# Decoder layer on one core: every engine keeps the source's order around the down projection, its weights are asked for two flushes ahead, and the next matrix's first four units go chunk by chunk

## The chip, the cores and the metric

One NeuronCore of a Trainium2 chip. The metric is the device time of one launch in microseconds (us); the kernel before was run three times, 2031.71, 2032.97 and 2035.16 us, median 2032.97.

## The reference: what is computed

One layer over 1056 tokens (a prompt of 1024 and 8 samples of 4), width 1024, in float32:

```
x = x + 1/2 * SwiGLU_1(RMSNorm(x))          # D_FF = 2816; gate, up, down
z = RMSNorm(x) @ w_in                       # q | k | v | gate B | gate C | h
x = x + concat([attention, short conv]) @ w_out
x = x + 1/2 * SwiGLU_2(RMSNorm(x))
x = x + sigmoid(RMSNorm(x) @ w_ple_gate) * (p @ w_ple_proj)
```

The parts around the change are the two down projections, and what follows each: `w_in` behind the first, `w_ple_gate` behind the second.

## The kernel before

**Numbers.** Each float32 operand is split into a high part (a cast on ACT) and a low part (a subtraction on DVE); a product is three matmuls, high x high, low x high, high x low. The gated matrices go through a scheme of seven products per 2x2 block of operands ("operations", in the order 1, 5, 2, 6, 7, 3, 4), so operands and results are also summed in blocks.

**Gate and up.** `gate_up` walks 22 column blocks j, each in two token halves c. A `segment` gives PE the seven products of a block (L446 to L448) and beside them drains the block before: casts, tanh (L578), products with the gate (L579, L600 to L605, on DVE, and L602 on POOL). The results' sums and splits (`hop_steps`, and `hop_last` for the last pair) go to a DRAM buffer `hop`.

**Down.** Two gate-up blocks make a pair, eleven in all; a pair comes back from `hop` as seven tiles of 528 KB (`load`, L875, by POOL's DMA queue) into four slots. FLUSH cuts the 44 products of a row block with a pair into 17 flushes of one to three pairs; each flush runs in two token halves (`DownQuad`, L828 to L830) and its results are added into X, on ACT the first time (L837), later on DVE (L839). A flush's weights (`DownWeights`) are four DMAs on SP's queue (L793), four sums on POOL (L797 to L800) and seven splits (ACT cast L364, DVE subtraction L365). They are asked for, summed and split in the second half of the flush ahead. In eight of the 17 flushes POOL also adds the residual into two rows of X (L882).

**Behind it.** The rows of X that are done are squared and summed, and their normalised splits are made (`prep`, L296 on ACT and L297 on DVE). The next matrix goes in units of 1024 columns: DMA to `wraw` (L172), cast (L182, ACT), subtraction (L183, DVE), then `proj` (L336 to L338) over three token chunks. `norm_r` sums the squares (L312 to L316), runs a chain of small DVE operations for the inverse root (L255 to L265), spreads it over the partitions with matmuls (L324) and hands it to k, v and q (L1092, L1132, L1157).

**The order.** All of it is written in Python in one order, but a scheduler inside the tile framework, with its own estimate of times, sets the order of the instructions of each engine. An engine works through its list in that order; a waiting instruction holds up all behind it.

Of the kernel before, what the change touches and what calls it, by code (L numbers as in the profile page):

```python
# [14 lines left out]
P = 128  # L15
# [6 lines left out]
FF = 22  # L22
# [48 lines left out]
DRAW = 42496  # L71

# [27 lines left out]
def tile_decoder_layer(  # L100
# [67 lines left out]
    def pump_dma():  # L168
        while st["dma"] < st["end"] and st["dma"] < st["split"] + RAW:
            i = st["dma"]  # L170
            t = at("wraw", (URAW2 if 2 <= i < 26 else URAW)[i % 2], 1024)
            nc.sync.dma_start(out=t, in_=units[i])  # L172
            raws[i] = t
            st["dma"] += 1
# [29 lines left out]
    def tick(split=True):  # L204
        now[0] += 1
        if split and can_split():
            split_one()
        while queue and min(queue)[0] <= now[0]:
            run_first()

# [324 lines left out]
    def hop_last(pr, c, src):  # L535
# [5 lines left out]
        def parts(u, n, hi, t, neg=False):  # L541
# [11 lines left out]
            lambda: parts(3, 2, new(), cell["a"]),  # L553
            lambda: parts(5, 2, new(), cell["b"], True),
# [54 lines left out]
    def lead_group(w, j, c, g):  # L609
# [20 lines left out]
        for h in range(2):  # L630
            ps = halfmm(1, h)
            nc.vector.tensor_tensor(out=g[:, h], in0=ps[:, :HH], in1=g[:, h], op=ALU.mult)
            if h:
                nc.sync.dma_start(out=hd[j, :, c * HC:(c + 1) * HC], in_=g.rearrange("p i t -> p (i t)"))
            yield

# [90 lines left out]
    def gate_up(gu, g, lw, steps, down):  # L727
# [36 lines left out]
        for j in range(LEAD, FF):  # L764
            for c in range(2):
                q = GateUp(w, j, c)
                if c:
                    q.follow = w = Weights(gu, j + 1) if j + 1 < FF else down.weights(0)
# [17 lines left out]
    class DownWeights(Weights):  # L786
        def __init__(self, dn, row, p0, p1):
            n = self.n = (p1 - p0) * P
            r = []
            for i in range(4):  # L790
                t = at("dr", DRAW + 384 * (dn_[0] % 6), 384)[:, :n]
                dn_[0] += 1
                nc.sync.dma_start(out=t, in_=dn[row, i, :, p0 * P:p1 * P])  # L793
                r.append(t)
# [71 lines left out]
    class Down:  # L866
# [3 lines left out]
        def weights(self, i):  # L870
            return DownWeights(self.dn, *FLUSH[i])
# [12 lines left out]
        def first(self, q):  # L884
# [7 lines left out]
            else:  # L892
                q.then = {
                    3: [lambda: ld(2, 1, 5, 2, 6)],
                    4: [lambda: ld(2, 7, 3, 4)],
                }

        def run(self, prev):
            w = prev.follow
# [36 lines left out]
            segment(None, prev)  # L936

# [93 lines left out]
    def norm_hook(g, xm):  # L1031

        def hook(r, ch):
            for m in (r, r + 4):
                for c in ((0,), (1, 2))[ch]:
                    square(c, m)
                if ch == 0:
                    prep(0, m, g)
                elif xm:
                    nc.sync.dma_start(out=xm_d[:, m], in_=X[m])  # L1040
            if r == 0 and ch == 1:
                for c in (1, 2):
                    for k in KORD:
                        prep(c, k, g)
        return hook

    dp = Down(w1d, xin, norm_hook(GM, True), 2)
    dp.run(gate_up(w1gu, G1, lw1, chunk1_steps(G1), dp))
    st["end"] = 26

# [100 lines left out]
    nc.gpsimd.memset(msq, 1.0)  # L1151
# [188 lines left out]
    nst = [norm_r(c, "nm", 9) for c in range(3)]  # L1340
    for c in range(3):
        ps = proj(U0, c)
        nst[c][0]()
        if c == 2:
            wdone(U0)
        ps1 = proj(U0 + 1, c)
        nst[c][1]()
        k_evac(c, ps)
        tick()
        v_evac(c, ps1)  # L1350
        tick()
    wdone(U0 + 1)
    for i in range(4):
# [4 lines left out]
        wdone(U0 + 2 + i)  # L1358

# [150 lines left out]
    dp = Down(w2d, xs_d, norm_hook(GP, False), 28)  # L1510
    dp.run(gate_up(w2gu, G2, lw2, chunk1_steps(G2), dp))
    st["end"] = 34
# [25 lines left out]
    for m in range(4):  # L1538
        ple_proj(m)
    nst = [norm_r(c, "np", 9) for c in range(3)]  # L1540
    for c in (0, 1):
        for m in (0, 1):
            ple_gate(m, c)
            nst[c][m]()
    ple_gate(0, 2)
    wdone(UG)
    nst[2][0]()
    for c in (0, 1):
        ple(0, c)
    ple_gate(1, 2)  # L1550
    wdone(UG + 1)
    nst[2][1]()
    ple(0, 2)
    for c in range(3):
        ple(1, c)
    for m in range(2, 8):
# [109 lines left out]
```

## Time and profile before

| | us |
|---|---|
| runs: lowest, median, highest | 2031.71, 2032.97, 2035.16 |
| the profiled execution's own time | 2034.04 |
| its span in the trace | 2032.3 |
| PE, DVE, ACT, POOL busy | 1955.5, 1375.5, 769.4, 912.6 |
| granted TensorE clock, mean | 0.978 |

The first down projection runs from 526 to 795 us, the second from 1683 to 1945. The span is what the trace covers; 1.7 us lie outside it. Busy shares are averages over stages with different limits, and what counts is which wait ends last in a stage.

### The profile page before, as it was taken

To read this page: it belongs to the slowest core of one execution; us is meant where nothing else is said; L and a number is where in the kernel's file an instruction comes from. 1 tells how busy PE (TensorE), PEld (TensorE's weight loads), DVE (VectorE), ACT (ScalarE), POOL (GpSimd) and SP (SyncE) were. 2 spreads that over 40 slices of the span, in tenths; PEclk is the share of its full clock that TensorE was granted. 3 is DMA by queue.
4 is the path that set the end of the run, shared out by engine and by line. 5 is a ranking of instruction groups with operands and counts; after the bars stand their busy time and mean duration, and the time that the engine had idled before them with its cause. 6 is when DMAs were issued, how large, how long until landed. Compare 5 with 4: busy or idle time off the path is not lost.

```text
span 2032.3 us, 38555 instructions
## 1 busy us (share of the span) xinstructions
PE 1955.5 (96%) x14639; PEld 1904.3 (94%) x14639; DVE 1375.5 (68%) x2571; ACT 769.4 (38%) x1654; POOL 912.6 (45%) x912
## 2 busy tenths in 40 slices
PE   7999999999899997999999799999999998999999
PEld 7999999999799997999887799999999997999998
DVE  6848877776467686456685357588777764777864
ACT  5324444444332233313344233344444434322521
POOL 2426665655456464002221125366565555565500
PEclk7999999999899998999999899999999999999999
DMA  6225754454988735101012331365445469986231
GB/s 240 85 67 189 244 168 143 136 165 132 365 293 265 242 117 173 35 22 33 31 32 86 106 105 48 113 214 183 138 152 163 127 222 317 295 295 194 93 128 50
DMA packets 189548, 315.46 MB, mean 155 GB/s; under 512 B 20801, under 2 KB 121545, under 8 KB 189236
## 3 DMA queue, kind: packets, MB, share of 16 engines
q1 hardware_dynamic: 164852, 224.55, 34.5%
q0 software_dynamic: 23648, 87.28, 12.6%
q8 instruction: 115, 1.88, 0.4%
q10 hardware_dynamic: 864, 1.18, 0.2%
q14 instruction: 69, 0.57, 0.1%
HBM read 204.66 MB, written 109.99 MB: 155 GB/s over the span
## 4 chain that ended last, share of the span: by engine, by line
PE 82%; DMA 6%; DVE 6%; issue 2%; POOL 2%; ACT 1%; SPq 0%; DVEq 0%; POOLq 0%; ACTq 0%
PE ps L446 11%; PE ps L447 11%; PE ps L448 11%; PE ps L828 7%; PE ps L830 7%; PE ps L829 7%; PE ps L336 4%; PE ps L338 4%; PE ps L337 4%; PE ps L1388 2%; PE ps L1389 2%; PE ps L1387 2%; PE ps L620 2%; PE ps L619 2%; PE ps L621 2%
## 5 line engine op out<-in xcount | busy, mean ns | idle before, releaser
L446 PE MATMUL ps<-bh_a,wh_a 128*128 128x264 f32 x2128 | 602.9, 285 | 4.7 <-DVE g_a L600 2.1
L447 PE MATMUL ps<-bh_a,wl_a 128*128 128x264 f32 x2128 | 604.3, 285 | 0.0
L448 PE MATMUL ps<-bl_a,wh_a 128*128 128x264 f32 x2128 | 599.6, 284 | 0.0
L446 PEld LDWEIGHTS ps<-bh_a,wh_a 128*128 128x128 f32 x2128 | 399.1, 188 | 7.4 <-DVE g_a L600 3.2
L447 PEld LDWEIGHTS ps<-bh_a,wl_a 128*128 128x128 f32 x2128 | 400.0, 188 | 0.0
L448 PEld LDWEIGHTS ps<-bl_a,wh_a 128*128 128x128 f32 x2128 | 399.9, 189 | 0.0
L828 PE MATMUL ps<-pair_a,vh_a 128*128 128x264 f32 x1232 | 355.9, 292 | 25.2 <-ACT x_a L837 8.8
L829 PE MATMUL ps<-pair_a,vl_a 128*128 128x264 f32 x1232 | 353.3, 288 | 0.0
L830 PE MATMUL ps<-pair_a,vh_a 128*128 128x264 f32 x1232 | 352.8, 288 | 0.0
L828 PEld LDWEIGHTS ps<-pair_a,vh_a 128*128 128x128 f32 x1232 | 234.6, 191 | 31.7 <-ACT x_a L837 10.3
L829 PEld LDWEIGHTS ps<-pair_a,vl_a 128*128 128x128 f32 x1232 | 236.4, 192 | 0.3 <-DVE vl_a L365 0.2
L830 PEld LDWEIGHTS ps<-pair_a,vh_a 128*128 128x128 f32 x1232 | 235.3, 191 | 0.0
L839 DVE SCALAR_TENSOR_TENSOR x_a<-ps,x_a 128x264 f32<-128x264 f32 x412 | 171.3, 425 | 90.4 <-PE ps L830 79.1
L336 PE MATMUL ps<-xnh_a,whi_a 128*128 128x384 f32 (+1 forms) x528 | 174.6, 331 | 12.9 <-DVE x_a L1479 7.0
L337 PE MATMUL ps<-xnh_a,wlo_a 128*128 128x384 f32 (+1 forms) x528 | 172.7, 328 | 0.0
L338 PE MATMUL ps<-xnl_a,whi_a 128*128 128x384 f32 (+1 forms) x528 | 172.7, 329 | 0.0
L365 DVE TENSOR_TENSOR wl_a<-ws_a,wh_a 128x512 fp32r<-128x512 f32 x152 | 131.8, 867 | 35.7 <-ACT wh_a L364 35.2
L389 POOL TENSOR_TENSOR ws_a<-wr_a,wr_a 128x512 f32<-128x512 f32 x38 | 50.8, 1336 | 213.0 <-DMA wr_a<-in_w2gu_dram 82.7
L364 ACT CAST wh_a<-ws_a 128x512 fp32r<-128x512 f32 x152 | 94.4, 621 | 99.9 <-PE ps L448 86.5
L364 ACT CAST vh_a<-dws_a 128x384 fp32r<-128x384 f32 (+2 forms) x136 | 63.1, 467 | 171.7 <-PE ps L830 139.2
L365 DVE TENSOR_TENSOR wl_a<-wr_a,wh_a 128x512 fp32r<-128x512 f32 x114 | 108.5, 954 | 12.8 <-ACT wh_a L364 11.6
L336 PEld LDWEIGHTS ps<-xnh_a,whi_a 128*128 128x128 f32 x528 | 102.0, 193 | 15.9 <-DVE x_a L1479 8.6
(268 smaller groups left out, 4166.8 us busy)
## 6 DMA issues: line engine op xcount, KB each, us to landing
pair_a<-hop POOLq DMA_DIRECT2D x154, 528.0 KB, 7.6
hop<-sg_a SPq DMA_DIRECT2D x240, 264.0 KB
wr_a<-in_w1gu_dram SPq DMA_DIRECT2D x88, 256.0 KB
wr_a<-in_w2gu_dram SPq DMA_DIRECT2D x88, 256.0 KB
hop<-sge_a SPq DMA_DIRECT2D x80, 132.0 KB
wraw_a<-in_win_dram SPq DMA_DIRECT2D x18, 512.0 KB
dr_a<-in_w1d_dram SPq DMA_DIRECT2D x44, 192.0 KB
dr_a<-in_w2d_dram SPq DMA_DIRECT2D x44, 192.0 KB
```

Source lines behind the costliest of these rows:

```text
L336: nc.tensor.matmul(ps[:, :W], lhsT=wh, rhs=xh, start=(k == 0), stop=False)
L337: nc.tensor.matmul(ps[:, :W], lhsT=wl, rhs=xh, start=False, stop=False)
L338: nc.tensor.matmul(ps[:, :W], lhsT=wh, rhs=xl, start=False, stop=(k == n - 1))
L364: nc.scalar.copy(out=hi, in_=src)
L365: nc.vector.tensor_tensor(out=lo, in0=src, in1=hi.bitcast(F32), op=ALU.subtract)
L446: nc.tensor.matmul(ps[:, :HH], lhsT=wh[:, ks], rhs=bh, start=(start and k == 0), stop=False, skip_group_check=True)
L447: nc.tensor.matmul(ps[:, :HH], lhsT=wl[:, ks], rhs=bh, start=False, stop=False, skip_group_check=True)
L448: nc.tensor.matmul(ps[:, :HH], lhsT=wh[:, ks], rhs=bl, start=False, stop=last, skip_group_check=True)
L828: nc.tensor.matmul(ps[:, :HH], lhsT=wh[:, ks], rhs=bh, start=(start and i == 0), stop=False, skip_group_check=True)
L829: nc.tensor.matmul(ps[:, :HH], lhsT=wl[:, ks], rhs=bh, start=False, stop=False, skip_group_check=True)
L830: nc.tensor.matmul(ps[:, :HH], lhsT=wh[:, ks], rhs=bl, start=False, stop=(i == n - 1), skip_group_check=True)
L839: nc.vector.scalar_tensor_tensor(out=x, in0=ps[:, :HH], scalar=f, in1=x, op0=ALU.mult, op1=ALU.add)
```

## The change

Between the first half of the last gate-up block and the end of the next matrix's first units, the scheduler is switched off: each engine gets its instructions as the Python code writes them (`in_order`). So that this order is usable, several things move in the code: a flush's weight DMAs go out two flushes ahead (flush 0 into four tiles of its own, `dr0`), apart from their sums; pairs 2 and 3 are loaded in the second halves of flushes 0 and 2 operation by operation, in place of the end of gate-up and of flush 0; the last pair's source is loaded a flush earlier and its last split delayed by five steps; the first unit of the next matrix is asked for after flush 15, and four units are in flight in place of two. The four first units are then worked as chunk 0 of all four, chunk 1, chunk 2 (`first_units`), in place of unit by unit; the splits of chunks 1 and 2 of X move from the end of the last flush into it. Line numbers shift by up to 72.

```diff
+            t = at("wraw", 30624 if i in (0, 26) else (URAW2 if 4 <= i < 26 else URAW)[i % 2], 1024)
...
             lambda: parts(3, 2, new(), cell["a"]),
+            *[lambda: None] * 5,
             lambda: parts(5, 2, new(), cell["b"], True),
...
+                if j == FF - 1 and c == 0:
+                    in_order(True)
                 if j == FF - 1:
                     down.first(q)
+                    if c:
+                        down.w[0].sums()
+                        down.w[1] = down.weights(1)
                 segment(q, prev)
                 prev = q
+                if j == FF - 2 and c:
+                    down.w = {0: down.weights(0)}
...
-            else:
-                q.then = {
-                    3: [lambda: ld(2, 1, 5, 2, 6)],
-                    4: [lambda: ld(2, 7, 3, 4)],
-                }
...
                     if c and i + 1 < len(FLUSH):
-                        nxt = self.weights(i + 1)
-                    done = (lambda r=f[0], c=c: self.hook(r, c)) if last_row[f[0]] == i else None
+                        nxt = self.w[i + 1]
+                        nxt.sums()
+                    done = (lambda r=f[0], c=c: self.hook(r, c)) if last_row[f[0]] == i and f[0] else None
                     q = DownQuad(w, c, f, done)
                     if c:
                         q.follow = nxt
+                        if i in (0, 2):
+                            for o in UNITS:
+                                q.then[o] = [lambda pr=2 + i // 2, o=o: self.load(pr, o)]
...
+                    if i in (4, 5) and c:
+                        src = from_hd(10, i - 4)
                     if i in (5, 6) and c == 0:
-                        hops.extend(hop_last(10, i - 5, from_hd(10, i - 5)))
+                        hops.extend(hop_last(10, i - 5, src))
+                    if i == len(FLUSH) - 1 and c:
+                        q.then[2] = [split_one]
...
-                    if i == 0 and c:
-                        self.load(3, 1, 5, 7, 2, 6, 3, 4)
-                    if i == len(FLUSH) - 1:
-                        if c == 0:
-                            st["end"] = self.end
-                            pump_dma()
-                        else:
-                            split_one()
+                    if c and i + 2 < len(FLUSH):
+                        self.w[i + 2] = self.weights(i + 2)
+                    if (i, c) in ((len(FLUSH) - 2, 1), (len(FLUSH) - 1, 0)):
+                        st["end"] = self.end - 3 * c
+                        pump_dma()
                 w = nxt
             segment(None, prev)
+            self.hook(0, 0)
+            split_one()
+            self.hook(0, 1)
...
+    def first_units(U, name, g, evac):
...
+        a = group(0, 0)
+        nst[0][0]()
+        split_next()
+        b = group(1, 0)
+        nst[0][1]()
+        preps(1, 0)
+        evac(0, 0, a)
+        evac(1, 0, b)
+        split_next()
+        a = group(2, 0)
+        preps(1, 1)
+        nst[1][0]()
+        evac(2, 0, a)
+        a = group(3, 0)
+        nst[1][1]()
+        evac(3, 0, a)
+        for u in range(4):
+            a = group(u, 1)
...
+    first_units(U0, "nm", GM, kvq_evac)
...
+    in_order(False)
```

Three places show the moved instructions; a row is line, operation, output and inputs (a name, its address, its number) and size.

First, ACT as the first down projection starts. Before: `sgl` is the cast of the last pair's source, which comes by DMA into `hd0`; `th` is the tanh of the last gate-up block; `x_a` is a down result; `vh` are weight splits.

```order
L364 CAST vh_a33728_6111<-dws_a41344_6017 128x128
L837 ACTIVATE x_a0_72<-ps_6153 128x264
L364 CAST vh_a34752_6177<-dws_a41728_6018 128x128
L364 CAST vh_a39424_6206<-dws_a42112_6019 128x128
L837 ACTIVATE x_a0_72<-ps_6153 128x264
L364 CAST sgl_a40192_6896<-hd0_6892 128x264
L578 ACTIVATE th_a48720_626<-g_a47664_1041 128x264
L364 CAST vh_a32704_6232<-dr_a43648_6014 128x128
```

The same place now:

```order
L370 CAST vh_a33728_6121<-dws_a41344_6019 128x128
L585 ACTIVATE th_a48720_626<-g_a47136_897 128x264
L869 ACTIVATE x_a0_72<-ps_6163 128x264
L370 CAST vh_a34752_6187<-dws_a41728_6020 128x128
L869 ACTIVATE x_a0_72<-ps_6163 128x264
L585 ACTIVATE th_a48720_626<-g_a47664_1041 128x264
L370 CAST vh_a39424_6216<-dws_a42112_6021 128x128
L370 CAST vh_a32704_6234<-dr0_a8304_5891 128x128
```

The cast `sgl` stood ahead of the last tanh; it now stands 67 rows behind it.

Second, POOL at the same place. Before: `pair_a` are the tiles of the pairs, their address telling pair and operation (23232 to 29568 and 44800, 45856 are pairs 2 and 3; 12672 and 13728 are operations 3 and 4 of pair 0); `dws` are the weight sums.

```order
L602 TENSOR_TENSOR g_a46608_779<-g_a46608_779,u_5932 128x264
L875 DMA pair_a23232_6210<-hop_76 128x1056
L875 DMA pair_a24288_6212<-hop_76 128x1056
L875 DMA pair_a44800_6297<-hop_76 128x1056
L875 DMA pair_a19008_6074<-hop_76 128x1056
L875 DMA pair_a20064_6076<-hop_76 128x1056
L875 DMA pair_a25344_6214<-hop_76 128x1056
L875 DMA pair_a26400_6216<-hop_76 128x1056
L798 TENSOR_TENSOR dws_a41344_6017<-dws_a40960_6016,dr_a42496_6008 128x128
L799 TENSOR_TENSOR dws_a41728_6018<-dr_a42496_6008,dr_a43264_6012 128x128
L875 DMA pair_a45856_6299<-hop_76 128x1056
L875 DMA pair_a12672_6131<-hop_76 128x1056
```

The same place now:

```order
L609 TENSOR_TENSOR g_a46608_779<-g_a46608_779,u_5942 128x264
L829 TENSOR_TENSOR dws_a40960_6018<-dr0_a8176_5889,dr0_a8304_5891 128x128
L830 TENSOR_TENSOR dws_a41344_6019<-dws_a40960_6018,dr0_a7920_5885 128x128
L831 TENSOR_TENSOR dws_a41728_6020<-dr0_a7920_5885,dr0_a8176_5889 128x128
L832 TENSOR_TENSOR dws_a42112_6021<-dws_a41344_6019,dr0_a8048_5887 128x128
L907 DMA pair_a19008_6084<-hop_76 128x1056
L907 DMA pair_a20064_6086<-hop_76 128x1056
L609 TENSOR_TENSOR g_a47136_897<-g_a47136_897,u_6081 128x264
L907 DMA pair_a12672_6141<-hop_76 128x1056
```

Six loads of pairs 2 and 3 stood ahead of tile 12672 and now stand behind; the four sums stand together and ahead of the loads.

Third, DVE as the first unit of `w_in` meets the norm. Before: `wlo` are low parts of units, `pms` and `pr` the start of the inverse-root chain.

```order
L297 SCALAR_TENSOR_TENSOR xnl_a40128_9064<-x_a0_72,vec_78,xnh_a39744_9056 128x384
L297 SCALAR_TENSOR_TENSOR xnl_a17184_9093<-x_a0_72,vec_78,xnh_a16896_9085 128x288
L183 TENSOR_TENSOR wlo_a32704_9254<-wraw_a6144_9210,whi_a31680_9253 128x1024
L183 TENSOR_TENSOR wlo_a34752_9261<-wraw_a7168_9216,whi_a33728_9260 128x1024
L316 TENSOR_SCALAR pms_9193<-ps_9192 128x3
L183 TENSOR_TENSOR wlo_a41536_9014<-wraw_a6144_9210,whi_a40512_9013 128x1024
L255 TENSOR_SCALAR pr_9164<-pms_9193 128x3
```

The same place now:

```order
L303 SCALAR_TENSOR_TENSOR xnl_a11136_8519<-x_a0_72,vec_78,xnh_a10752_8511 128x384
L185 TENSOR_TENSOR wlo_a15872_9048<-wraw_a43584_8955,whi_a14848_9047 128x1024
L1224 MEMSET msq_a14656_9110 128x72
L318 MEMSET pms_9142 128x3
L322 TENSOR_SCALAR pms_9142<-ps_9141 128x3
L261 TENSOR_SCALAR pr_9113<-pms_9142 128x3
L267 SCALAR_TENSOR_TENSOR nt_9148<-pr_9113 128x3
```

The chain stood behind the low parts of units 2, 3 and 4 (the last of them between its first two steps); it now stands behind that of unit 1.

## Rows read from the trace of the kernel before

**Rows 1.** The page's line of granted clock, 40 slices of the span, in tenths.
```profile
PEclk7999999999899998999999899999999999999999
```

**Rows 2.** Windows: us, busy PE (x), PEld, DVE, ACT, POOL, clock, DMA share, GB/s.
```profile
520.00:580.00 60.00, 48.30 (x328) 46.11 (x327) 28.44 (x58) 23.64 (x63) 33.95 (x45) 0.86 0.89 303
580.00:640.00 60.00, 60.00 (x494) 60.00 (x493) 43.85 (x79) 16.02 (x33) 32.70 (x42) 1.00 0.90 288
...
760.00:780.00 20.00, 19.10 (x138) 18.63 (x138) 19.99 (x36) 13.00 (x27) 16.08 (x23) 1.00 0.52 158
780.00:800.00 20.00, 14.99 (x96) 14.76 (x94) 8.93 (x14) 6.56 (x11) 6.99 (x9) 0.94 0.63 206
800.00:820.00 20.00, 15.24 (x90) 14.57 (x91) 8.77 (x42) 3.64 (x8) 0.00 (x0) 0.72 0.36 112
...
1676.00:1736.00 60.00, 50.68 (x365) 47.96 (x364) 32.49 (x67) 26.02 (x70) 36.06 (x48) 0.94 0.90 301
...
1856.00:1916.00 60.00, 58.16 (x476) 57.96 (x475) 49.88 (x98) 22.96 (x53) 33.72 (x35) 1.00 0.34 113
...
1940.00:1960.00 20.00, 18.02 (x116) 17.93 (x115) 9.84 (x41) 4.01 (x6) 0.00 (x0) 0.91 0.23 77
1960.00:1980.00 20.00, 18.95 (x121) 18.72 (x120) 13.53 (x27) 5.84 (x11) 0.00 (x0) 1.00 0.42 127
```

**Rows 3.** Waits of PE, 490 to 600 us: total us, times, longest.
```profile
PE ps L828 <- ACT x_a L837: 4.2, 2, 2.2
PE ps L828 <- DVE g_a L605: 3.4, 1, 3.4
PE ps L828 <- DMA pair_a<-hop: 3.4, 2, 2.5
```

**Rows 4.** Timeline, 526 to 533 us: start, length, engine, line, idle before.
```profile
528.76 0.41 ACT L364 CAST sgl_a<-hd 128x264 fp32r<-128x264 f32 x1 [2.30 <-DMA hd<-hd]
...
530.96 0.39 PE L828 MATMUL ps<-pair_a,vh_a 128*128 128x264 f32 x1 [3.45 <-DVE g_a L605]
```

**Rows 5.** Chain that ended last, 500 to 560 us: start, length, what.
```profile
524.82 14.09 DMA pair_a<-hop
```

**Rows 6.** Timeline of POOL, 498 to 545 us.
```profile
540.67 0.72 POOL L799 TENSOR_TENSOR dws_a<-dr_a,dr_a 128x256 f32<-128x256 f32 x1
```

**Rows 7.** Waits of PE, 740 to 860 us.
```profile
PE ps L324 <- DVE pms L312: 8.4, 1, 8.4
```

**Rows 8.** Waits of all engines, 770 to 860 us.
```profile
ACT whi_a L182 <- DMA wraw_a<-in_win_dram: 11.5, 3, 7.6
```

**Rows 9.** Timeline of DVE, 780 to 806 us.
```profile
800.22 1.22 DVE L183 TENSOR_TENSOR wlo_a<-wraw_a,whi_a 128x1024 fp32r<-128x1024 f32 x1 [3.40 <-ACT whi_a L182]
801.36 0.16 DVE L255 TENSOR_SCALAR pr<-pms 128x3 int32<-128x3 int32 x1
```

**Rows 10.** Waits of all engines, 1660 to 1740 us.
```profile
ACT vh_a L364 <- DMA dr_a<-in_w2d_dram: 4.7, 2, 3.9
```

**Rows 11.** Groups of DVE by shape, 500 to 860 us: busy us, mean ns.
```profile
L365 DVE TENSOR_TENSOR vl_a<-dr_a,vh_a 128x384 fp32r<-128x384 f32 x33 | 34.3, 1040 | 5.2 <-ACT vh_a L364 4.1
```

**Rows 12.** Groups of POOL by shape, 500 to 780 us.
```profile
L882 POOL TENSOR_TENSOR x_a<-x_a,res 128x528 f32<-128x528 f32 x16 | 22.8, 1435 | 5.3 <-DVE x_a L839 5.2
L800 POOL TENSOR_TENSOR dws_a<-dws_a,dr_a 128x384 f32<-128x384 f32 x11 | 13.5, 1223 | 0.8 <-issue 0.6
...
L797 POOL TENSOR_TENSOR dws_a<-dr_a,dr_a 128x384 f32<-128x384 f32 x11 | 11.5, 1050 | 30.7 <-DMA dr_a<-in_w1d_dram 28.5 <-DVE x_a L839 2.2
```

**Rows 13.** Timeline of DVE, 1864 to 1871 us.
```profile
1865.85 3.57 DVE L365 TENSOR_TENSOR vl_a<-dr_a,vh_a 128x384 fp32r<-128x384 f32 x1
...
1870.96 0.54 DVE L365 TENSOR_TENSOR vl_a<-dr_a,vh_a 128x384 fp32r<-128x384 f32 x1
```

**Rows 14.** Timeline of POOL, 1862 to 1872 us.
```profile
1866.36 2.59 POOL L882 TENSOR_TENSOR x_a<-x_a,res 128x528 f32<-128x528 f32 x2
```

**Rows 15.** Waits of PE, 1865 to 1872 us.
```profile
PE ps L828 <- DVE x_a L839: 1.8, 1, 1.8
```

More of the change, by code (lines that the diff above doesn't have):

```diff
@@ L71 @@
 DRAW = 42496
+W0AT = 7920
 FRAG = [1056 * k + 528 for k in (0, 4, 1, 5, 2, 6, 3)]
@@ L635, in lead_group, with in_order @@
             yield
+    manual = []
+    def in_order(on):
+        if on:
+            manual.append(tc.manual_schedule())
+            manual[-1].__enter__()
+        else:
+            manual.pop().__exit__(None, None, None)
     nacc = [None, None]
@@ L767, in gate_up @@
                 if c:
-                    q.follow = w = Weights(gu, j + 1) if j + 1 < FF else down.weights(0)
+                    q.follow = w = Weights(gu, j + 1) if j + 1 < FF else down.w[0]
                 assert not hops
@@ L786, in tile_decoder_layer, with __init__, sums @@
     class DownWeights(Weights):
-        def __init__(self, dn, row, p0, p1):
+        def __init__(self, dn, i):
+            row, p0, p1 = FLUSH[i]
             n = self.n = (p1 - p0) * P
[L789 to L794, printed above, removed]
+            self.r = []
+            for b in range(4):
+                if i == 0:
+                    t = at("dr0", W0AT + P * b, P)
+                else:
+                    t = at("dr", DRAW + 384 * (dn_[0] % 6), 384)[:, :n]
+                    dn_[0] += 1
+                nc.sync.dma_start(out=t, in_=dn[row, b, :, p0 * P:p1 * P])
+                self.r.append(t)
+        def sums(self):
+            n, r = self.n, self.r
             s = [at("dws", DWS + 384 * i, 384)[:, :n] for i in range(4)]
@@ L1034, in hook, with preps, group @@
             for m in (r, r + 4):
-                for c in ((0,), (1, 2))[ch]:
-                    square(c, m)
                 if ch == 0:
                     prep(0, m, g)
-                elif xm:
+            for c in ((0,), (1, 2))[ch]:
+                for m in (r, r + 4):
+                    square(c, m)
+            if ch and xm:
+                for m in (r, r + 4):
                     nc.sync.dma_start(out=xm_d[:, m], in_=X[m])
[L1041 to L1044, printed above, removed]
-        return hook
-    dp = Down(w1d, xin, norm_hook(GM, True), 2)
+        return hook
+    def first_units(U, name, g, evac):
+        nst = [norm_r(c, name, 9) for c in range(3)]
+        def preps(c, n):
+            for k in KORD[4 * n:4 * n + 4]:
+                prep(c, k, g)
+        def group(u, c):
+            ps = proj(U + u, c)
+            if c == 2:
+                wdone(U + u)
+            tick(c == 2)
+            return ps
+        a = group(0, 0)
[16 more added lines that the diff above has]
+            a = group(u, 1)
+            if u < 2:
+                preps(2, u)
+            if u in (1, 2):
+                nst[2][u - 1]()
+            evac(u, 1, a)
+        for u in range(4):
+            evac(u, 2, group(u, 2))
+    dp = Down(w1d, xin, norm_hook(GM, True), 4)
     dp.run(gate_up(w1gu, G1, lw1, chunk1_steps(G1), dp))
-    st["end"] = 26
     mix = [at("mix", MIXAT[c], KT * CW[c]).rearrange("p (k w) -> p k w", k=KT) for c in range(3)]
@@ L1337, in later, with kvq_evac @@
             after(t0 + d, fn)
[L1340 to L1353, printed above, removed]
+    def kvq_evac(u, c, ps):
+        if u == 0:
+            k_evac(c, ps)
+        elif u == 1:
+            v_evac(c, ps)
+        else:
+            q_evac(u - 2, c, ps)
+        if u == 1 and c == 1:
+            st["end"] = 26
+    first_units(U0, "nm", GM, kvq_evac)
+    for i in range(2, 4):
         for c in range(3):
@@ L1509, in tile_decoder_layer @@
     rbs.clear()
-    dp = Down(w2d, xs_d, norm_hook(GP, False), 28)
+    dp = Down(w2d, xs_d, norm_hook(GP, False), 30)
     dp.run(gate_up(w2gu, G2, lw2, chunk1_steps(G2), dp))
-    st["end"] = 34
     UG = UNIT["wpg"]
@@ L1536, in ple, with gate_evac @@
         nc.sync.dma_start(out=yT[:, m * NT + CS[c]:m * NT + CS[c] + W], in_=x)
-    for m in range(4):
-        ple_proj(m)
[L1540 to L1556, printed above, removed]
+    ple_proj(0)
+    def gate_evac(m, c, ps):
+        pgate[m, c] = ps
+        if c == 0 and m < 3:
+            ple_proj(m + 1)
+        if m == 3 and c == 0:
+            st["end"] = 34
+        ple(m, c)
+    first_units(UG, "np", GP, gate_evac)
+    in_order(False)
+    for m in (4, 5):
+        ple_proj(m)
+    for m in range(4, 8):
         if m + 2 < 8:
```

10 lines of the change are left out of this document (6 added, 4 removed).

## The prediction, made before the run

> **What bounds the kernel now.** I read the clock line of the page first, then the windows around each place where it dips, then the waits of PE in those windows, then the timelines of the engines named there.
>
> The clock line stands at full speed nearly everywhere; behind the cold start it dips in slices 11, 16 and 23 of 40 [rows 1], each of 51 us. Slice 11 is the start of the first down projection and slice 16 its end, where the change is; slice 23 lies in the attention. In full flow a window of 60 us reads 494 matmuls, 0.1215 us apart, with PE busy all of it [rows 2]. The start of the first down projection reads 328, 166 short, so 166 x 0.1215 = 20.2 us are lost there; the start of the second reads 365, 129 short, 15.7 us [rows 2]. The first transition, from the end of the down projection to `w_in`, has PE idle for 0.90 + 5.01 + 4.76 = 10.7 us in three windows, and a lower clock that costs 0.06 x 14.99 + 0.28 x 15.24 = 5.2 us, 15.9 in all; the second has 1.98 + 1.05 idle and 0.09 x 18.02 of clock, 4.6 us [rows 2]. Together 56 us, in stages where PE has work but not its inputs. All else that I looked at runs with PE full, and there no order of the other engines can be worth anything.
>
> Why PE waits there:
> - At the first start PE waits for down results on ACT (4.2 us), for a product on DVE (3.4) and for pair tiles (3.4) [rows 3], 11 us in all; idle time in the window is 60 - 48.3 = 11.7, and the clock, 0.86 over 48.3 us of work, makes another 6.8 [rows 2]. Idle and clock are 18.5 of the 20.2.
> - The 3.4 us on DVE begin on ACT: the cast of the last pair's source waited 2.30 us for its DMA, the tanh of the last gate-up block stood behind it, and PE waited 3.45 us for what followed [rows 4].
> - Pair tiles: the chain runs 14.09 us through one load in DMA [rows 5]. In the order before, six loads of pairs 2 and 3, not needed for tens of us, stand ahead of operations 3 and 4 of pair 0.
> - At the first transition one wait of 8.4 us holds PE [rows 7]. The spread needs the inverse-root chain on DVE; its second step began at 801.36, straight behind a unit's low part that had waited 3.40 us on ACT [rows 9], which waited 11.5 us in three pieces for that stage's raw units [rows 8]. In the order before, that unit is the third of three ahead of this step.
>
> **The change, part by part.** PE's arithmetic is the same: as many matmuls and bytes, so only waits move.
>
> *Start of the first down projection.* The cast moves 67 rows back on ACT, so the 3.4 us go. The six loads move behind pair 0. At 303 GB/s [rows 2] a load of 528 KB (540,672 bytes) takes 1.78 us, so six are 10.7 us; operations 3 and 4 of pair 0 would land that much earlier, more than the 3.4 us that PE waits for them [rows 3]. The weight sums stood behind loads too (the first of flush 1 ran at 540.67 [rows 6], 14 us after PE's first down product at 526); they now stand ahead of the loads of pair 2, on tiles asked for a half block earlier or more, which takes the cause from much of the 4.2 us on ACT, whose casts wait for sums. With 11 us of waits gone PE has no reason to drop to 1.2 GHz, which was granted here behind these waits, and the 6.8 us of clock go too. What is late next: the weights of flush 2, asked for at the end of flush 0, are wanted half a flush later. At the second start ACT waited for such weights 4.7 us, at most 3.9 [rows 10]; I leave 5 us for this and for what remains of the waits on ACT. 20 - 5 = 15 us gained; bounds 10 (weights and pairs each keep a wait as they have now) and 20 (nothing is late).
>
> *Start of the second.* The same, from 15.7 us with 9.3 idle and 0.06 x 50.68 = 3.0 of clock [rows 2]; 5 left, so 11 gained, between 7 and 15.
>
> *First transition.* The chain now stands behind unit 1's low part, whose data are asked for during the last flush. Chunk by chunk, 4 groups of 24 matmuls lie between the need for unit 1 and that of chunk 1, so each unit has a group's time (24 of about 0.16 us, from 90 in 15.24 us [rows 2], or 4 us) for its DMA, cast and subtraction. The wait of 8.4 us and the clock behind it go. Left: the splits of chunk 1 and 2 that move here must keep pace, and unit 3 comes late by a us or two, as its raw place is shared. 13 gained of 15.9, bounds 0 and 15.9.
>
> *Second transition.* 4.6 us, of which the order can save those behind the last products; 2 gained, bounds 0 and 4.6.
>
> *Source order within the flushes.* Here a cost can arise that was not there. POOL now gets a flush's four sums, then two residual additions, back to back: 3 x 1.05 + 1.22 + 2 x 1.435 = 7.2 us [rows 12] (all sums but the last taken at the row's 1.05), while a half flush of three pairs lasts 63 x 0.1215 = 7.65 us. Beside it DVE makes seven splits and nine or so additions; a split of this shape has a mean of 1.04 us [rows 11] and lasted 0.54 with POOL quiet [rows 13]. Now and then it is far longer: 3.57 us, beginning half a us before the two residual additions of 2.59 us [rows 13, 14], and PE then waited 1.8 us [rows 15]. The stretch in which this fell lost 18 matmuls in all (476 against 494 [rows 2]), 2.2 us, with four flushes with residuals in it. In the new order a split can meet such a run as before; the order no longer avoids it nor seeks it. In the other direction the fixed order frees POOL's sums from waiting pair loads. I take -3 us over both projections, between -8 (four such events of 2 us more than today) and +4 (today's 2.2 us in each projection go).
>
> For this the Trainium skill has a rule, SBUF — State Buffer, section "Who interferes with whom": a DVE instruction with two SBUF inputs contends with a GpSimd instruction that reads SBUF, and whoever issues first holds the shared port pair for its whole instruction. The trace agrees in the 3.57 us above, though most splits beside sums only stretch to about 1 us. By the rule's plain wording every split beside POOL would be blocked; that is the third rival below.
>
> *Sum.* 15 + 11 + 13 + 2 - 3 = 38 us. The profiled execution took 2034.04; 2034 - 38 = 1996. The median of the runs is 1.07 us under that execution, so I predict 1995 us. The bounds: 10 + 7 + 0 + 0 - 8 = 9 us gained, 2024; 20 + 15 + 15.9 + 4.6 + 4 = 59, 1974.
>
> **The rivals.**
> 1. *The DMA engines bind at the starts.* For it: they are busy 0.89 to 0.90 in both windows of the first start at 303 and 288 GB/s [rows 2], and the bytes don't get fewer; if PE goes faster, the loads of pairs 2 and 3 are wanted sooner. Against: PE ran full for 60 us at the same share. Then the starts gain half, 7.5 + 5.5 in place of 26: 2034 - 25 - 1 = 2008 us.
> 2. *The transitions gain nothing.* The units' low parts and the splits of chunks 1 and 2, all on DVE, now lie between the groups, where PE could wait for them in turn. Against: DVE was busy 8.93 and 8.77 of 20 us there [rows 2]. The loss of 15 us makes 2034 - 23 - 1 = 2010.
> 3. *Slower: splits blocked by POOL's runs.* In each half flush in which sums are made, 16 in each projection, POOL's four sums and the residual additions start together, at the same point at which DVE starts its splits. If the source order makes each of these 32 lose what the one event cost, 1.8 us [rows 15], that is 58 us: 2034 - (15 + 11 + 13 + 2) + 58 - 1 = 2050. It decides from 41 / 32 = 1.3 us a half flush on. For it: POOL's run fills a half flush where there are residuals. Against: only 16 of the 32 have them, and in the order before the sums lay beside the splits too, with PE full in 580 to 640 us [rows 2].
> 4. *No change.* The waits are for data that come no earlier (the last pair's source, raw units), whatever stands ahead: 2033 us. Against: two of the waits were shown to start in an instruction that the engine didn't have to do yet.
>
> **How the numbers follow.** The forecast 0.60, rival 1 0.14, rival 2 0.08, rival 3 0.13, no change 0.05. Faster by over 0.2% (about 4 us, what a measurement of this kernel can tell from no change): 0.60 + 0.14 + 0.08 and 0.01 of the fourth, 0.83. Same 0.04, slower 0.13. The range: from 1978, near the low bound, to 2024, the high bound of the sum, which takes in rivals 1 and 2 and leaves out rivals 3 and 4. The forecast's own range is 1980 to 2010.
>
> **What would show it.** In the profile of the changed kernel the first 60 us of the first down projection should read over 440 matmuls at a clock of 0.95 or more, and those of the second over 450; the wait of L828 for the product of the last gate-up block should be gone, and that for pair tiles under 1 us. At the first transition the spread's wait should be under 2 us and the clock full. Waits of POOL's sums for `dr` at flush 2 would show what I left. In the flushes, a window of 60 us of the middle should read 485 or more; 470 or fewer throughout, with splits of 2 us and more beside POOL, would be rival 3. The prediction is wrong if pair tiles hold PE at the starts as now, or if the lost matmuls turn up again in flushes 3 to 15.

## The result, and the profile after

| | before | changed |
|---|---|---|
| median of the runs, us (lowest to highest, runs) | 2034.07 (2031.71 to 2035.55, 4) | 2019.6 (2018.04 to 2022.41, 4) |
| profiled execution, its span, us | 2034.04, 2032.3 | 2018.56, 2016.8 |
| granted TensorE clock, mean | 0.978 | 0.984 |

The ratio is 0.9931, 95% interval 0.9914 to 0.9949: faster by 14 us. The direction and the range held; the size did not: I forecast 38 us.

Counted by its products (L828 to L830, now L860 to L862), the first projection ran from 520.2 to 780.6 us before and runs from 517.1 to 767.8 now, the second from 1678.1 to 1933.9 and now from 1660.6 to 1909.0. (The times of the projections given with the profile before, 526 to 795 and 1683 to 1945, begin and end later than its products.)

The clock line of the changed kernel's page, to be read against [rows 1]: slices 11 and 16 are now full, the dip of slice 23 (attention) now lies in 22 and 23.

```profile
PEclk8999999999999999999998899999999999999999
```

Windows of the changed kernel (the second projection starts 17.5 us earlier than before); columns as in [rows 2].

```profile
520.00:580.00 60.00, 57.13 (x460) 56.10 (x459) 38.23 (x73) 25.68 (x66) 36.30 (x48) 1.00 0.90 310
580.00:640.00 60.00, 57.94 (x469) 57.27 (x469) 44.53 (x85) 17.22 (x34) 37.48 (x45) 1.00 0.96 315
...
700.00:760.00 60.00, 53.67 (x409) 52.59 (x408) 42.77 (x87) 21.28 (x49) 30.05 (x31) 0.94 0.30 103
...
780.00:800.00 20.00, 18.59 (x124) 17.83 (x122) 12.19 (x42) 8.68 (x18) 9.81 (x19) 1.00 0.45 130
800.00:820.00 20.00, 18.24 (x119) 17.62 (x120) 9.50 (x39) 6.71 (x13) 0.00 (x0) 0.91 0.21 72
...
1660.00:1720.00 60.00, 57.14 (x463) 56.34 (x462) 36.43 (x72) 26.15 (x69) 35.66 (x48) 1.00 0.93 321
...
1840.00:1900.00 60.00, 53.69 (x430) 52.60 (x430) 45.72 (x92) 22.05 (x49) 32.54 (x33) 1.00 0.29 95
...
1920.00:1940.00 20.00, 16.44 (x85) 15.96 (x84) 15.70 (x38) 8.77 (x18) 0.00 (x0) 0.83 0.31 95
```

The starts read 460 and 463 matmuls in place of 328 and 365, at full clock. But 580 to 640 us, full before, now reads 469, and the late flushes read 409 (at a clock of 0.94) and 430, where [rows 2] has 476 for the second projection and the trace before, for the first, has 477:

```profile
700.00:760.00 60.00, 58.66 (x477) 58.20 (x477) 49.35 (x98) 21.71 (x49) 34.80 (x39) 1.00 0.48 162
```

To see where the time went flush by flush I worked out from the starts of the matmuls what PE loses: for each matmul, the time to the start of the next, less the lower quartile of that time for its shape, so that waits and a lower clock both count. The sums are by place: the matmuls of the down projection are counted off in order of time, 21 for each pair of a half flush (a "b" is a flush's second half). In us:

| place | before | changed |
|---|---|---|
| flushes 0 to 2, first / second projection | 20.7 / 14.3 | 4.4 / 4.4 |
| flush 5b | 0.2 / 0.3 | 2.6 / 2.5 |
| flushes 6 to 11 | 1.9 / 1.9 | 3.0 / 3.6 |
| flush 12b | 2.0 / 2.2 | 2.8 / 2.8 |
| flushes 13 and 14 | 0.6 / 0.5 | 2.2 / 2.2 |
| flush 15b | 0.1 / 0.1 | 6.1 / 3.5 |
| flushes 3 to 16 together | 7.3 / 8.4 | 20.0 / 17.9 |
| first 450 matmuls behind the first, 300 behind the second | 18.1 / 5.4 | 9.1 / 7.1 |

The starts gave back 16.3 and 10.0 us, the first transition 9.0; flushes 3 to 16 took 12.7 + 9.5 = 22.2, the second transition 1.6. The sum is 11.5. The 4 us to the two spans' 15.5 lie elsewhere: 3.1 of them before the first projection, mostly in the first 80 us, which the change does not touch. They are a difference between executions: in the profiles of the changed kernel and of its edits below the first projection starts anywhere from 516.6 to 521.1 us.

The waits of PE over the first projection (520 to 770 us) are nearly all of one kind:

```profile
PE ps L860 <- DVE x_a L871: 11.9, 12, 2.9
PE ps L860 <- ACT vh_a L370: 0.7, 1, 0.7
```

They are 12.6 of the 24.4 us that the table has for it; a part of the rest is the clock (below). Gone are the waits for the last gate-up block's product and for pair tiles [rows 3], and the spread's 8.4 us [rows 7]. What is late now is a down result on DVE (L871 is before's L839). The longest case, in flush 15b of the first projection, over the timelines of POOL, ACT, DVE and PE in order of time:

```profile
743.20 2.91 POOL L291 TENSOR_TENSOR acc_a<-acc_a,sq 128x384 f32<-128x384 f32 x3 [0.60 <-ACT sq L290]
746.07 0.72 POOL L829 TENSOR_TENSOR dws_a<-dr_a,dr_a 128x256 f32<-128x256 f32 x1
746.82 0.41 ACT L370 CAST vh_a<-dws_a 128x256 fp32r<-128x256 f32 x1 [2.49 <-POOL dws_a L829]
747.26 0.61 DVE L371 TENSOR_TENSOR vl_a<-dws_a,vh_a 128x256 fp32r<-128x256 f32 x1 [1.81 <-ACT vh_a L370]
747.79 1.23 DVE L871 SCALAR_TENSOR_TENSOR x_a<-ps,x_a 128x264 f32<-128x264 f32 x3
748.83 0.56 PE L860 MATMUL ps<-pair_a,vh_a 128*128 128x264 f32 x1 [2.94 <-DVE x_a L871]
```

Read upward: PE waited 2.94 us for a result, which stood on DVE behind a split, whose cast waited on ACT for the weight sum, which stood on POOL behind additions of the norm's squares. In the source the squares come first, so in the fixed order they do too.

The same wait of 2.94 us stands in flush 15b of both projections, but the half flush loses 6.1 us in the first and 3.5 in the second. The windows around the two waits show why:

```profile
745.00:750.00 5.00, 2.06 (x11) 1.89 (x12) 3.16 (x8) 1.12 (x3) 3.98 (x6) 0.80 0.33 112
750.00:755.00 5.00, 5.00 (x26) 5.00 (x25) 2.45 (x6) 2.06 (x4) 1.50 (x2) 0.52 0.02 3
...
1888.00:1893.00 5.00, 2.06 (x16) 1.72 (x15) 3.16 (x8) 1.39 (x4) 4.84 (x7) 1.00 0.00 0
1893.00:1898.00 5.00, 5.00 (x43) 5.00 (x43) 4.59 (x11) 2.42 (x5) 1.92 (x3) 1.00 0.36 108
```

In the first the granted clock fell during the wait to the lower of its two levels (0.52 of full speed from 750 to 755 us, 26 matmuls), in the second it stayed full (43 matmuls).

### The profile page after: what moved, and what is told of

Its sections match the earlier page's. It is cut to its first block, busy times and chain, and to the rows that moved or that the text cites. A ratio compares the mean times of both kernels' runs of the same rounds, so it can differ in the third digit from the quotient of the medians.

```text
span 2016.8 us, 38417 instructions
## 1 busy us (share of the span) xinstructions
PE 1947.3 (97%) x14639; PEld 1892.7 (94%) x14639; DVE 1378.3 (68%) x2572; ACT 770.8 (38%) x1654; POOL 918.1 (46%) x911
## 3 DMA queue, kind: packets, MB, share of 16 engines
q0 software_dynamic: 23648, 87.28, 12.8%
## 5 line engine op out<-in xcount | busy, mean ns | idle before, releaser
L860 PE MATMUL ps<-pair_a,vh_a 128*128 128x264 f32 x1232 | 356.1, 289 | 25.8 <-DVE x_a L871 24.2
L862 PE MATMUL ps<-pair_a,vh_a 128*128 128x264 f32 x1232 | 351.8, 286 | 0.0
L860 PEld LDWEIGHTS ps<-pair_a,vh_a 128*128 128x128 f32 x1232 | 233.2, 189 | 34.0 <-ACT vh_a L370 12.3
L871 DVE SCALAR_TENSOR_TENSOR x_a<-ps,x_a 128x264 f32<-128x264 f32 x412 | 170.3, 426 | 104.2 <-PE ps L862 79.9
L862 PEld LDWEIGHTS ps<-pair_a,vh_a 128*128 128x128 f32 x1232 | 232.7, 189 | 0.0
L907 POOL DMA_DIRECT2D pair_a<-hop x154 | 82.8, 544 | 84.0 <-PE ps L862 76.2
L371 DVE TENSOR_TENSOR wl_a<-wr_a,wh_a 128x512 fp32r<-128x512 f32 x114 | 108.1, 949 | 12.6 <-ACT wh_a L370 11.6
```

Source lines behind the costliest of these rows:

```text
L371: nc.vector.tensor_tensor(out=lo, in0=src, in1=hi.bitcast(F32), op=ALU.subtract)
L860: nc.tensor.matmul(ps[:, :HH], lhsT=wh[:, ks], rhs=bh, start=(start and i == 0), stop=False, skip_group_check=True)
L862: nc.tensor.matmul(ps[:, :HH], lhsT=wh[:, ks], rhs=bl, start=False, stop=(i == n - 1), skip_group_check=True)
L871: nc.vector.scalar_tensor_tensor(out=x, in0=ps[:, :HH], scalar=f, in1=x, op0=ALU.mult, op1=ALU.add)
```

## The experiments

Line numbers are the changed kernel's, but where an edit shifts them (with the scheduler on, L856 is its L860; in the order alone, L808 is before's L797). "Theory A": in a fixed order a waiting instruction holds those behind it on its engine. "Theory B" is what my third rival became: POOL and DVE in each other's way. "Loses" is the measure of the table above.

**Squares behind the weight sums.**

```
-  done = (lambda ...: self.hook(r, c)) if ...
+  done = (lambda ...: held.append((r, c)) if c else self.hook(r, c)) if ...
...
   nxt.sums()
+  while held: self.hook(*held.pop(0))
```

> The changed kernel, in which the squares of the norm of a half flush (ACT squares, POOL additions) are written behind the weight sums of the next flush in place of ahead of them. Theory A: in flush 15 the fixed order sets four POOL additions of squares, which wait for results, ahead of the weight sums; the splits wait for the sums, the down results stand behind the splits on DVE, PE stalls and its clock falls. Then the second half of flush 15 loses under 1 us in each projection in place of 6.1 and 3.5, and the time is 8 us under the changed kernel's, near 2011.5. Theory B: POOL and DVE are in each other's way wherever both work on SBUF; the same POOL work lies beside the same splits, the loss stays within 1.5 us of what it was, and the time is 2018 to 2021.

2013.05 us (2012.76 to 2014.74), ratio to before 0.9894 (0.9873 to 0.9916). Flush 15b loses 1.3 and 1.3 us in place of 6.1 and 3.5, and flushes 13 and 14 1.4 in place of 2.2. POOL's timeline:

```profile
743.10 0.92 POOL L829 TENSOR_TENSOR dws_a<-dr_a,dr_a 128x256 f32<-128x256 f32 x1
...
746.64 4.18 POOL L291 TENSOR_TENSOR acc_a<-acc_a,sq 128x384 f32<-128x384 f32 x4
```

The same additions, 4.18 us of them, now run beside the same splits and cost little: theory A for this place; 6.5 us. The edit moves ACT's squares too; that POOL was the link rests on the cast's wait of 2.49 us for the sum, above.

**Residual additions behind the half flush.**

```
-  else:
-      for fn in res: fn()
   segment(q, prev)
+  if c:
+      for fn in res: fn()
```

> The changed kernel, in which the residual additions of a flush are written behind its second half in place of ahead of it, so that POOL makes them beside a first half, in which DVE has three splits in place of four and more slack. Theory B: the eight second halves with residuals in each projection lose 6.2 us in the first; beside sums alone they would lose 0.2 to 0.4 each, so 3 to 4 us come back in each projection, the second half of flush 12 falls from 2.75 to under 1 us, and the time is 6 to 8 us shorter, near 2012.5. Theory A alone: residual additions stand behind all sums on POOL, and nobody waits for them but results of a later flush: no change, 2018 to 2021.

2019.09 us (2013.51 to 2021.96), ratio 0.9919 (0.9893 to 0.9946): not told apart from the changed kernel. Flush 13b falls from 1.04 to 0.15 us in both projections, but 12b stays at 2.76. Theory B is right about 13b, 1.8 us in all, and not about 12b. Flush 5b falls too, to 1.8 and 1.25 us.

**The scheduler left on, all moves kept** (`in_order` does nothing).

> The changed kernel with the scheduler left on: all that moved in the code stays moved, the order is the scheduler's. If the gain at the two starts (16.3 and 10.0 us) is owed to the fixed order (cast behind the tanh, loads of pairs 2 and 3 behind pair 0), more than half of it is lost again, and the losses in flushes 3 to 16 (22 us more than before) go: about 2034 - 9 at the first transition - 22 + ... = 2015 to 2025. If the gain at the starts is owed to what moved in the code (weights asked for earlier, loads later), the starts keep it and the time falls to 2000 or less.

2018.9 us, but 2011.57 to 2027.36; ratio 0.9909 (0.9877 to 0.9942), the changed kernel's time within what can be told. Its profile is that of the slowest run, so it tells places rather than sizes: flushes 0 to 2 lose 12.8 and 13.1 us, 3 and 4 lose 6.9 and 7.7 (0.7 in the changed kernel), 15b 0.4 and 0.4, the 450 matmuls behind the first projection 10.0 and the 300 behind the second 0.7. ACT's timeline and, below it, a wait of PE from 515 to 600 us show what came back:

```profile
529.57 0.41 ACT L370 CAST sgl_a<-hd 128x264 fp32r<-128x264 f32 x1 [4.87 <-DMA hd<-hd]
529.89 0.42 ACT L585 ACTIVATE th_a<-g_a 128x264 f32<-128x264 f32 x1
```

```profile
PE ps L856 <- DVE g_a L612: 3.6, 1, 3.6
```

The cast stands ahead of the tanh again, with the weights asked for early all the same. Of the first start's gain the moves alone keep about half, of the second's little, and in this execution flushes 3 and 4 lose that again; the fixed order makes the rest, and gives it away in flushes 5 to 16.

Behind the projections it is the other way round: the moves alone bring the whole gain of the first transition (10.0 us left, 9.1 in the changed kernel), and behind the second 0.7 is left where the fixed order leaves 7.1. With flush 16 taken in, the second reads 3.8 us with the scheduler on, 9.4 in the changed kernel and 6.8 before. Its window there, roughly the counterpart of 1920 to 1940 us above, and below it the longest wait of the changed kernel's PE in the same place (1895 to 1980 us), for a unit:

```profile
1940.00:1960.00 20.00, 20.00 (x126) 19.97 (x125) 12.96 (x44) 4.63 (x9) 0.00 (x0) 1.00 0.16 58
```

```profile
PE ps L342 <- ACT whi_a L184: 2.8, 1, 2.8
```

So the loss there belongs to the fixed order. One difference in PE's own list: 41 matmuls of the next matrix lie among those of flush 16 here, 44 in the kernel before, none in the fixed order. What that is worth was not tried by itself.

**The order alone**: the kernel before with the scheduler off over the same stretch, nothing moved.

> The kernel before with the scheduler off over the same stretch and nothing moved in the code. Every flush asks for its weights at the start of the half in which they are split: with POOL's first sum waiting for its DMA (some 4 to 8 us), each second half flush of 7.65 us loses 3 us or more, 16 times in each projection: over 100 us slower than before, 2130 or more. If the order alone were the gain, it would be near 2020.

2136.85 us, ratio 1.0501 (1.046 to 1.0542). Waits, 520 to 880 us:

```profile
POOL dws_a L808 <- DMA dr_a<-in_w1d_dram: 57.3, 9, 16.0
```

The order without the moves costs 100 us. Late weights are the largest wait of POOL, but not all of it: in the same stretch PE also waited 14.0 us for a pair tile and 10.0 for the inverse-root chain.

**The last pair's split three steps later** (`*[lambda: None] * 8` for 5).

> The changed kernel with the last split of the last pair's sums three steps later (eight empty steps in place of five), about 3.3 us. Theory A (a waiting instruction in the fixed order holds those behind it): in flush 5 ACT waits 3.4 us for the tile that this split writes, DVE's subtraction waits for it, a down result stands behind, PE waits 1.1 us; with the tile free by then the second half of flush 5 falls from 2.6 and 2.5 to 1.3 us each, the time by 2.5 us, near 2017. Theory B (POOL beside DVE): the loss stays at 2.3 to 2.7.

2026.45 us (2021.92 to 2028.84), ratio 0.9961 (0.9947 to 0.9975): 7 us slower than the changed kernel, against the expectation. The aim was met, 5b falls to 1.25 in both projections; but flush 7b of the second rises from 0.9 to 8.0 us. POOL and PE there:

```profile
1769.48 0.99 POOL L829 TENSOR_TENSOR dws_a<-dr_a,dr_a 128x384 f32<-128x384 f32 x1 [7.40 <-DMA dr_a<-in_w2d_dram]
...
1772.91 0.56 PE L860 MATMUL ps<-pair_a,vh_a 128*128 128x264 f32 x1 [5.40 <-DVE x_a L871]
```

The weights of flush 8 came late. Their DMAs stand on SP's queue behind the stores of that split: the first was issued 1.55 us ahead of the start of flush 7, 0.4 us behind the last store, in place of 3.79 us ahead in the changed kernel. It is so in both projections, and in the run with all four edits (below), where the same stall followed in both; but in the first projection of this run 7b lost only 1.9 us. That the store's place on SP is the cause was not tried by itself, and the lateness alone does not set the size.

**The fourth unit split ahead of the first evacuations** (the operations that take finished products out of PSUM; `split_next()` above `preps(1, 0)`).

> The changed kernel with the fourth unit of the next matrix split ahead of the first evacuations and of the splits of chunk 1, in place of behind them. Theory A: behind the second projection ACT's cast of that unit stands behind activations that wait for DVE, and PE waits 2.8 + 0.8 us for it and runs slower after; these waits go, the stage behind the second projection falls from 7.3 to about 4 us, behind the first by 1: about 2015.5. The rival: DVE is the bound in this stretch, the splits of chunk 1 only come later, and nothing is gained: 2018 to 2021.

2019.53 us (2018.14 to 2022.25): no change. PE's wait for the unit went, another took its place (waits of PE, 1905 to 1990 us):

```profile
PE ps L330 <- DVE pr L271: 4.9, 1, 4.9
```

The spread of chunk 1 now waits for the inverse-root chain, which stands on DVE behind splits and evacuations. Two pieces of work were in the wrong place, and I had moved one.

**All four edits.**

> The changed kernel with all four edits: squares behind the weight sums, residual additions behind the half flush, the last pair's split later, the fourth unit earlier. If they add up: 6.5 + 0.5 + 2.5 + 4 us under the changed kernel's 2019.6, 2006. If DVE is simply full in these stretches, each gain is paid back in the next half flush: 2012 or more.

2016.43 us (2013.14 to 2020.02): they don't add up, since the third edit's stall comes with them (flush 7b 6.5 and 5.9 us).

**All four without weight sums, first try.**

> As the run with all four edits, with the four weight sums of each flush left out (the splits read raw tiles instead; the output is not the reference's). Theory B, in what is left of it: the sums on POOL stretch DVE's splits from 0.55 to 1.0 us and more, and this is the loss of 0.2 to 0.6 in each second half flush and of 2.75 in flush 12; without sums the flushes 3 to 16 lose under 4 us in each projection in place of some 11, the time 12 us under the run with the sums. The rival: seven splits and nine additions fill DVE in the shorter half flushes by themselves, flush 12 keeps over 2 us, and less than 5 us is gained.

2019.8 us (2013.07 to 2024.68). The edit missed its place: POOL still makes the sums in this run's trace. So it repeats the run with all four edits and says nothing on theory B; 3.4 us lie between the two medians.

**Without weight sums**, on the first two edits: `s = [r[3], r[0], r[2], r[1]]` for the four additions. The splits read raw tiles, so the output is not the layer's.

> The changed kernel with the squares behind the weight sums and the residual additions behind the half flush, and with the four weight sums of each flush left out (the splits read raw tiles in their place; the output is not the reference's). Theory B in what is left of it: the sums on POOL stretch DVE's splits from 0.55 to 1.0 us and more, and this is the 2.75 us of flush 12 and the 0.2 to 0.6 of the other second halves. Then flush 12 falls under 1 us, flushes 3 to 16 lose under 6 us in each projection in place of some 13, and the time is 12 us or more under that of the run with the sums. The rival: the splits and additions fill DVE in the shorter half flushes by themselves, flush 12 keeps over 2 us, and less than 5 us is gained.

2021.25 us (2019.96 to 2023.9), slower than the run with the sums (below, 2008.43). Raw tiles are now held until their splits, so later weights come late: flushes 0 to 2 lose 10.7 and 9.9 us. Flush 12b falls from 2.75 to 1.6 and 1.9, 5b from 2.55 and 1.25 to 0.8 and 0.1, and flushes 3 to 16 together lose what they lost (13.6 and 13.2 against 13.8 and 13.2), new stalls in flush 4b (2.1 each) among it. DVE's splits from 550 to 760 us, with the sums and then without:

```profile
L371 DVE TENSOR_TENSOR vl_a<-dws_a,vh_a 128x384 fp32r<-128x384 f32 x43 | 35.3, 822 | 5.0 <-ACT vh_a L370 4.8
L371 DVE TENSOR_TENSOR vl_a<-dr_a,vh_a 128x384 fp32r<-128x384 f32 x32 | 26.9, 844 | 2.3 <-ACT vh_a L370 1.2
```

```profile
L371 DVE TENSOR_TENSOR vl_a<-dr_a,vh_a 128x384 fp32r<-128x384 f32 x77 | 54.8, 716 | 11.1 <-ACT vh_a L370 7.7
```

Splits get shorter by 0.1 us without the sums. By this run sums beside splits cost about 1 us in each 12b and 1 to 2 in each 5b; as the edit made waits of its own, more can't be read from it.

**The first two edits together.**

> The changed kernel with the squares behind the weight sums and the residual additions behind the half flush, without the later split of the last pair, whose three steps moved a stall of 6 us into flush 7. If the two gains add up (6.5 and 0.5 us): near 2012.5, flush 13 and 14 under 1 us together, flush 7 under 1 us. If the residual additions collide elsewhere: 2015 or more.

2008.43 us (2006.81 to 2010.97), ratio to before 0.9882 (0.9864 to 0.9899): 11 us under the changed kernel, more than the 7 of the two alone; where the rest comes from was not traced.

**Four loads of pair 2 ahead of operations 3 and 4 of pair 0** (`q.then = {2: [ld(2, 1, 5)], 6: [ld(2, 2, 6)]}` in the second half of the last block).

> The changed kernel with four loads of pair 2 set ahead of operations 3 and 4 of pair 0 on POOL's queue, as six loads of pairs 2 and 3 were in the kernel before. If a load stands 1.8 us in the queue, operations 3 and 4 of pair 0, which land at 523.1 and 525.1 in the changed kernel, land 7 us later, PE waits some 3 us for them, and flushes 0 to 2 lose 8 us in place of 4.4 in each projection; the time is 4 to 8 us longer, 2024 to 2027. If the loads overlap in the DMA engines and the order in the queue does not matter: no change.

2026.59 us (2022.03 to 2029.26), 7 us slower, and flushes 0 to 2 lose 8.2 us in each projection: the sizes I expected, by another way. POOL, and PE's waits from 515 to 600 us:

```profile
540.61 0.72 POOL L829 TENSOR_TENSOR dws_a<-dr_a,dr_a 128x256 f32<-128x256 f32 x1 [8.33 <-DMA dr_a<-in_w1d_dram]
```

```profile
PE ps L860 <- DVE x_a L871: 4.5, 2, 2.8
PE ps L860 <- DMA pair_a<-hop: 0.6, 1, 0.6
```

Pair tiles hold PE for 0.6 us only. POOL's first sum for flush 2 waited 8.33 us for weights (8.18 in the second projection; 1.12 and 0.38 in the changed kernel), and the result behind the split held PE for 2.8. The early loads cost the weights, not pair 0.

**The two edits, the fourth unit earlier, and chunk 1's chain (`nst[1][0]()`) ahead of the evacuations.**

> The changed kernel with the squares behind the weight sums and the residual additions behind the half flush, and in the stage behind each projection the fourth unit split ahead of the first evacuations and the inverse-root chain of chunk 1 ahead of them too. If the stage behind the second projection lost its gain to the order on DVE (in the run with the fourth unit earlier alone, PE waited 4.9 us for that chain, which stood behind splits and evacuations), it falls from 7.8 to about 4 us, and the time is 3 to 4 us under that of the run without these two edits, near 2005. If DVE is full there whatever the order, the wait moves to the next group again and the time stays at 2007 to 2010.

2001.49 us (1999.91 to 2006.73), ratio to before 0.9832 (0.9809 to 0.9855): faster by 35 us than the kernel before, which read 2036.92 beside it, and 18 us under the changed kernel's median, the best version. The trace is of the slowest of its runs. In it the first 450 matmuls behind the first projection lose 7.5 us (11.0 in the run of the first two edits alone), the stage behind the second 6.4 in place of the 4 that I expected (7.8): the chain still holds PE there (waits of PE, 1895 to 1980 us), by 3.2 in place of 4.9 us:

```profile
PE ps L330 <- DVE pr L271: 3.2, 1, 3.2
```

## Why the prediction was wrong

- *Starts: right in size.* 15 and 11 forecast, 16.3 and 10.0 measured, with 4.4 us left in each, where I had set 5 aside. The cast ahead of the tanh was right (the run with the scheduler on). That the loads of pairs 2 and 3 hurt by holding up operations 3 and 4 of pair 0 was right in the kernel before [rows 3]: by their place in POOL's list the loads issued at 522.79 and 524.82 are those of operations 3 and 4, they landed at 536.89 and 538.90, and PE's two waits for pair tiles ended at 537.02 and 538.95. Set ahead again in the new order, they hurt by holding up flush 2's weights. Rival 1 fell: the DMA engines were 0.90 busy at 310 GB/s with PE at 460 matmuls.
- *First transition: 13 forecast, 9.0 measured.* The 8.4 us wait went as I said; the run with the scheduler on lost no more there, so the moves brought this gain. Of what is left, PE waited 1.8 us for DVE's statistics of q, 1.4 for a unit and 1.0 for a down result, and the clock dipped to 0.91; the rest is not assigned.
- *Second transition: 2 gained forecast, 1.6 lost.* Rival 2 was right here in its result: unit 3's cast stood on ACT behind activations that wait for DVE, and with that mended the chain on DVE was late. But it is the order, not the amount of work: with the scheduler on, the same work lost 3.8 us there, flush 16 included, in place of 9.4. The last run won back 0.9 of it against the changed kernel, and 1.6 behind the first.
- *Source order within the flushes: the step that failed.* I took -3 us, bounds -8 and +4; it was -22.2, and the lost matmuls turned up in flushes 3 to 16, as the prediction's own sign of being wrong says. I priced it by one event of the old order (a split beside two residual additions, [rows 13 to 15]) and asked only how often that would recur. It was another thing: I had not followed the norm's squares through POOL, where the source puts them ahead of the next flush's sums. By the runs, over both projections: the squares 8.5 us of loss (6.5 of time), 2.7 of them the clock in flush 15b of the first projection; residual additions 1.8 in 13b; the last pair's tile 2.6 in 5b (its cure costs more elsewhere, and the residual additions' edit took 2.1 off the same place). What is left of the rise against the kernel before, 2.1 in 5b and 1.3 in 12b, may be sums beside splits, by a run with new waits of its own. Some 6 us, spread over flushes 6 to 16 in pieces under 1.5, stay unassigned.
- *Rival 3* had the right sign for this term, the right engines and place, and the wrong mechanism and price: 1.8 us in each of 32 half flushes, where the loss sat in a few of them. Of the Trainium skill's rule on the shared port pair (SBUF — State Buffer, "Who interferes with whom") this case shows stretching on average, 0.82 to 0.84 against 0.72 us a split with and without sums, far from a block of whole instructions each time; 4.18 us of POOL additions beside splits left 1.3 us of loss. The split of 3.57 us, in which the prediction saw the rule, fits a hold but not the order of issue: it began at 1865.85, ahead of the additions at 1866.36 [rows 13, 14], and was held all the same.
- *A reading to set right:* PE's first down product began at 520.2 us, not at 526, so the first sum of flush 1 ran 20 us behind it and not 14. No term of the sum uses it.

Had the step been sized at 22, the sum would have been 2034 - 19 - 1 = 2014; the transitions' 7.6 us too many make it 2022, against 2019.6. That the range held is luck as far as this step goes: it lost far more than its own bound of 8 us, and the starts, near their forecast, made up for it.

## What to carry to other kernels

At the starts a fixed order beat the scheduler's, as far as one profile of each tells: the scheduler put a cast that waits for a DMA ahead of work that was ready; whether its estimate of the landing is the reason was not looked at. But a fixed order is only as good as the source's: walk every engine's list around each instruction that waits, those of side work (norms, residuals) first of all, and ask what stands behind it. An order needs the moves that make it usable: without them it cost 100 us here, while the moves with the scheduler's order did as well as the whole change, and better behind the second projection. A fixed order that ends where the projection ends was not tried. When a stall is cured, look for the next one on the same engine before counting the gain.

## What the runs showed of the hardware

A wait of PE can cost more than itself, by the clock: two waits of 2.94 us cost 6.1 us where the granted clock fell to 0.52 behind the wait and 3.5 where it stayed at 1.00. In flush 7b of the run with the later split, weights that came late made PE wait 5.4 us, the clock read 0.50 from 1772 to 1776 us, and the half flush lost 8.0.

Loads on POOL's queue delayed loads on SP's: with four pair tiles of 528 KB issued earlier, and the weight tiles of 128 KB for flush 2 issued as before, 7.2 to 10.6 us behind the start of flush 0 (first projection), POOL's sum waited 8.33 us for them, where it waited 1.12 us in the changed kernel.
